# Gate square roots and norm roots as powers on GpSimd, and a rebuilt first stage, in a two-layer decoder trunk on one core

## Chip, cores, metric

One core of one Trainium2 chip. The metric is the device time of one execution in microseconds (us), lower is better. The core has a matrix engine (PE), a vector engine (DVE), a scalar engine (ACT) that computes functions from loadable tables, GpSimd (POOL), and SP, which here only issues transfers from HBM.

## The reference

The input x has 256 rows of 1024. Layer 0 is a gated linear recurrence, layer 1 causal attention with 8 heads of 128 (one block of 256 keys, so plain causal softmax). Cut to what matters here:

```python
def _rmsnorm(x, g):
    y = xf * lax.rsqrt(jnp.mean(xf * xf, axis=-1, keepdims=True) + EPS)
    return (y * g.astype(jnp.float32)).astype(x.dtype)
...
    r = jax.nn.sigmoid((_block_diag(u, w_a) + b_a).astype(jnp.float32))
    gi = jax.nn.sigmoid((_block_diag(u, w_x) + b_x).astype(jnp.float32))
    log_a = -RG_C * r * jax.nn.softplus(-lam.astype(jnp.float32))
    a = jnp.exp(log_a)
    b_in = jnp.sqrt(-jnp.expm1(2.0 * log_a)) * (gi * u.astype(jnp.float32))
    _, hs = lax.associative_scan(_lin_combine, (a, b_in), axis=1)
    y = hs.astype(h.dtype) * jax.nn.silu(g)
    return y @ w_out
...
    x = x + gate[:, None, :] * y
```

Every sub-layer reads `RMSNorm(x) * (1 + scale(c)) + shift(c)`, where shift, scale and gate are products of silu(c) with `mod_w`. A last norm gives the output.

## The kernel before

All weights come through SP as 512 KB blocks in the order of the string `ORDER`, each into one of `NRAW` raw buffers. Every large product runs as three products of split numbers: `split_into` makes a rounded part (`hi`, a cast on ACT or DVE) and the rest (`lo`, a subtraction on DVE), and PE multiplies hi by hi, hi by lo and lo by hi into one PSUM bank.

The program is first recorded as a list of operations. A planner (`Plan`) gives each a cost from a formula, simulates the engines, and so sets the order of the instructions on each engine and, where an operation may run on either, whether ACT or DVE takes it. It tries 80 random variations of its priorities and keeps the best. The order on each engine is then fixed; semaphores do the rest.

The stages, with the names that the prediction uses:

- **First stage.** The two halves of x (`xr`) are squared and summed on ACT (`sq_a`), `rms` turns the sums into 1/root (`rv_a`, `rn_a`, `rt_a`, `ry_a`), `xn_a` is the normed half, and PE transposes it (`tp_a`). Meanwhile silu(c) is made from `c8` and the first 128 columns of shift and scale are computed by `mod_one` (banks `gvm0s`, `mc_m0s`, result `sg4m0s`). `mod_apply` forms h (`hrm`, `h_hi`, `h_lo`) and `u_rows` starts the product u = h W (bank `u`). `warm` matmuls fill PE before that.
- **Gates.** u is convolved (`uc`); two groups of four 128-channel slices (j = 0, 1) follow. PE makes `pa` and `px`, ACT the sigmoid (`rr`), tanh (`tx`), then Exp (`aq`, the decay a) and Tanh of p4 times r (`rr` again). With t that tanh, the factor under the root is proportional to t, and the root is applied to it, times (1 + a).
- **Scan and output.** DVE multiplies the root into `wgx`, runs four scans, multiplies with the SiLU path (`sg`), splits into `y_hi` and `y_lo`; PE multiplies with `wo` (bank `r_wo`). The gate row is spread over partitions by POOL (`gate_g`), and x1 follows.
- **Layer 1.** Norm `b`, the keys and values (`v`, `k`), attention, output product (`r_wp`), norm `f` and the output `ot`.

In the gates the root is a table function on ACT, followed by a product on DVE:

```python
        A.activation(qg, rr, AF.Sqrt, scale=0.0625)
        V.scalar_tensor_tensor(wg[:, js], ag, 1.0, wg[:, js], ALU.add, ALU.mult)
        V.tensor_mul(wg[:, js], qg, wg[:, js])
```

ACT holds one set of function tables at a time: Sigmoid, Sqrt, Ln and the set of Exp and Tanh each need an `ACT_TABLE_LOAD` when the function changes.

Of the kernel before, what the change touches and what calls it, by code (L numbers as in the profile page):

```python
# [10 lines left out]
F32 = mybir.dt.float32  # L11
# [15 lines left out]
NRAW = 11  # L27
NSPL = 4
NWARM = 16
NWARM2 = 4  # L30
SUM0 = 3
# [16 lines left out]
def blocks():  # L48
# [55 lines left out]

def packed(inputs):
# [14 lines left out]
class Plan:  # L120
# [7 lines left out]
    SETS = {AF.Exp: "e", AF.Tanh: "es", AF.Sigmoid: "s", AF.Sqrt: "q", AF.Ln: "l"}  # L128
# [157 lines left out]

    def _forward(self, urge):
# [12 lines left out]
        while len(seq) < n:  # L300
# [52 lines left out]
        return max(fin), start, eng, sorted(range(n), key=lambda i: (start[i], i))  # L353

# [7 lines left out]
    def order(self):  # L362
# [15 lines left out]
        rnd = random.Random(self.SEED)  # L378
        for _ in range(self.ROUNDS):
            part, far = rnd.choice((0.003, 0.01, 0.05, 0.3)), rnd.choice((500, 3000, 10000))  # L380
            other = [u + rnd.gauss(0, far) if rnd.random() < part else u for u in urge]
            got = self._forward(other)
            if got[0] <= best[0]:
                best, urge = got, other
# [8 lines left out]
    ROUNDS, SEED = 80, 4  # L393
# [35 lines left out]
def kernel(ctx: ExitStack, tc: tile.TileContext, x, c, mod_b, norm_g, rg_conv_w, rg_conv_b,  # L429
                       rg_b_a, rg_b_x, rg_lambda, kv_norm_g, kv_mod_b, final_norm_g, pack, out):  # L430
# [16 lines left out]
    x, c, out = x[0], c[0], out[0]  # L447
# [13 lines left out]
    def split_into(raw, hi, lo):  # L461
        plan.copy(hi, raw)
        V.tensor_sub(lo, raw, hi.bitcast(F32))


    def wsplit(name):
        while len(halves) <= windex[name]:
# [5 lines left out]
            split_into(t, hi, lo)  # L473
# [86 lines left out]
    th = const.tile([KT, P], F32, name="cth")  # L560
    A.activation(th, c8, AF.Tanh, scale=0.5)
    V.scalar_tensor_tensor(c8, th, 1.0, c8, ALU.add, ALU.mult)
    pt = bank("pt_c")
    PE.transpose(pt[:, 0:KT], c8, ident[0:KT, 0:KT])
    csB = const.tile([P, KT, 32], F32, name="csB")
    V.tensor_scalar(csB, pt[:, 0:KT].unsqueeze(2).broadcast_to([P, KT, 32]), 0.5, None, ALU.mult)
    csT = const.tile([P, KT], F32, name="csT")
    V.tensor_scalar(csT, pt[:, 0:KT], 0.5, None, ALU.mult)
# [3 lines left out]


    def rms(nm, parts, early=None):
        bias, nbias = eps, neps
        for i, row in enumerate(parts):
            w = row.shape[-1]
            sq = tmp.tile([P, w], F32, tag="xn" if w > 512 else "tg", name=f"sq_{nm}{i}")
            if early is not None and i == 0:
                A.activation(sq[0:early.shape[0], 0:1], early, AF.Sqrt, scale=0.0)  # L580
            ss = small.tile([P, 1], F32, tag="ss", name=f"ss_{nm}{i}", bufs=4)
            A.activation(sq, row, AF.Square, accum_out=ss)
            if i < len(parts) - 1:
                b = small.tile([P, 2], F32, tag="rb", name=f"rb_{nm}{i}", bufs=4)
                V.tensor_scalar(b[:, 0:1], ss, 1.0 / D, bias, ALU.mult, ALU.add)
# [201 lines left out]
    for k in range(2):  # L787
        mod_apply("m0", k, 1, m0s[k], xnT, h0_h, h0_l)
        u_rows(k)
# [353 lines left out]
```

## Time and profile before

| | us |
|---|---|
| median of 3 runs | 257.39 (257.09 to 258.31) |
| profiled execution | 257.7 |
| its span, first to last instruction | 255.7 |
| PE busy | 242.2 (95%) |
| DVE busy | 208.8 (82%) |
| ACT busy | 161.2 (63%) |
| POOL busy | 18.3 (7%) |

The profile is of one execution; 2.0 us of its time lie around the span. Busy PE includes filler matmuls. Idle time of an engine is put down to what released it.

### The profile page before, as it was taken

The numbers are of one execution on the slowest core, as the hardware profiler recorded it, in microseconds if no ns is written. First come the engines' busy times: TensorE is split into PE (matmuls) and PEld (weight loads), VectorE is DVE, ScalarE is ACT, GpSimd is POOL, SyncE is SP. The second block draws the span as 40 slices with busy tenths as digits, with TensorE's granted clock in tenths as the row PEclk, the third lists the DMA queues.
The fourth block names the chain that finished last, engine by engine and source line by source line (L and its number), as shares of the span: only waits on it lengthen the run. The fifth ranks groups of instructions, "written<-read, shape, count | busy, mean of one in ns | idle before, by whom it ended". The sixth has DMA issues, their size and how long they took to land.

```text
span 255.7 us, 4865 instructions
## 1 busy us (share of the span) xinstructions
PE 242.2 (95%) x1823; PEld 215.7 (84%) x1823; DVE 208.8 (82%) x378; ACT 161.2 (63%) x288; POOL 18.3 (7%) x31
## 2 busy tenths in 40 slices
PE   8899999999999996997999999999999999999970
PEld 7697799999897874865898898999999998889870
DVE  2773799899969999999898999973766789798483
ACT  7662755595799995079943385863537365786242
POOL 8100000000000033000000000010000000005030
PEclk9999999999999999999999999999999999999996
DMA  6999999992697879999999999986897520000003
GB/s 214 410 417 420 413 420 417 420 415 91 238 352 314 309 270 360 419 396 383 420 316 378 395 393 415 416 299 261 253 354 292 173 82 3 1 0 3 1 17 147
DMA packets 20695, 72.24 MB, mean 283 GB/s; under 512 B 2728, under 2 KB 3008, under 8 KB 20672
## 3 DMA queue, kind: packets, MB, share of 16 engines
q1 hardware_dynamic: 19840, 71.15, 71.9%
q0 software_dynamic: 688, 0.59, 0.9%
q8 instruction: 14, 0.23, 0.4%
q10 hardware_dynamic: 144, 0.20, 0.2%
q14 instruction: 9, 0.07, 0.1%
HBM read 70.87 MB, written 1.05 MB: 281 GB/s over the span
## 4 chain that ended last, share of the span: by engine, by line
PE 77%; ACT 12%; DVE 7%; issue 2%; DVEq 0%; ACTq 0%
PE u L409 9%; PE g L409 9%; PE v L409 9%; PE r_wp L409 6%; PE ga L409 5%; PE pj_wkb L409 5%; PE pj_wqb L409 5%; PE q L409 5%; PE k L409 4%; PE r_wo L409 3%; DVE x L409 3%; PE sc L409 3%; ACT L409 3%; PE warm L409 2%; PE pj_wgc L409 2%
## 5 line engine op out<-in xcount | busy, mean ns | idle before, releaser
L409 ACT ACT_TABLE_LOAD x14 | 18.0, 1283 | 1.0 <-PEq L1126 0.7
L409 PE MATMUL u<-h_lo,wu_hi 128*128 128x256 f32 x64 | 18.1, 285 | 0.0
L409 PE MATMUL u<-h_hi,wu_lo 128*128 128x256 f32 x64 | 18.1, 284 | 0.0
L409 PE MATMUL g<-h_hi,wgb_hi 128*128 128x256 f32 x64 | 18.0, 283 | 0.0
L409 PE MATMUL g<-h_lo,wgb_hi 128*128 128x256 f32 x64 | 18.0, 283 | 0.0
L409 PE MATMUL u<-h_hi,wu_hi 128*128 128x256 f32 x64 | 17.8, 288 | 0.0
L409 PE MATMUL g<-h_hi,wgb_lo 128*128 128x256 f32 x64 | 17.8, 283 | 0.0
L409 DVE SCALAR_TENSOR_TENSOR maccg<-g,csT,maccg 128x1024 f32<-128x1024 f32 x12 | 15.3, 1278 | 1.3 <-DMA g<-in_pack_dram 1.3
L409 POOL DMA_DIRECT2D row_g<-gsg x8 | 4.6, 582 | 142.1 <-issue 142.1
L409 PE MATMUL r_wp<-wp_hi,o_hi 128*128 128x512 f32 (+1 forms) x40 | 14.6, 364 | 0.0
L409 PE MATMUL r_wp<-wp_lo,o_hi 128*128 128x512 f32 (+1 forms) x40 | 14.2, 354 | 0.0
L409 PE MATMUL r_wo<-wo_hi,y_hi 128*128 128x512 f32 x32 | 12.4, 397 | 1.6 <-ACT y_hi L169 1.6
L409 PE MATMUL r_wp<-wp_hi,o_lo 128*128 128x512 f32 (+1 forms) x40 | 13.8, 350 | 0.0
L409 PE MATMUL v<-wv_hi,hk_hi 128*128 128x512 f32 x32 | 12.3, 394 | 1.3 <-ACT hk_hi L169 1.3
L409 PE MATMUL r_wo<-wo_hi,y_lo 128*128 128x512 f32 x32 | 12.3, 394 | 0.4 <-DVE y_lo L409 0.4
L409 DVE TENSOR_TENSOR wgb_lo<-wgb,wgb_hi 128x1024 fp32r<-128x1024 f32 x8 | 9.8, 1222 | 3.5 <-ACT wgb_hi L169 3.5
L409 PEld LDWEIGHTS u<-h_lo,wu_hi 128*128 128x128 f32 x64 | 12.2, 191 | 0.4 <-issue 0.4
L409 PEld LDWEIGHTS u<-h_hi,wu_lo 128*128 128x128 f32 x64 | 12.2, 191 | 0.4 <-issue 0.4
L409 PE MATMUL v<-wv_lo,hk_hi 128*128 128x512 f32 x32 | 12.5, 391 | 0.0
L169 ACT CAST wgb_hi<-wgb 128x1024 fp32r<-128x1024 f32 x8 | 8.4, 1048 | 6.3 <-PE g L409 3.7
L409 PE MATMUL r_wo<-wo_lo,y_hi 128*128 128x512 f32 x32 | 12.4, 397 | 0.0
L409 PEld LDWEIGHTS g<-h_hi,wgb_hi 128*128 128x128 f32 x64 | 12.3, 192 | 0.0
(306 smaller groups left out, 868.6 us busy)
## 6 DMA issues: line engine op xcount, KB each, us to landing
g<-in_pack_dram SPq DMA_DIRECT2D x16, 512.0 KB, 5.0
wu<-in_pack_dram SPq DMA_DIRECT2D x8, 512.0 KB, 10.0
wo<-in_pack_dram SPq DMA_DIRECT2D x8, 512.0 KB, 6.5
mkh<-in_pack_dram SPq DMA_DIRECT2D x8, 512.0 KB, 6.3
mkc<-in_pack_dram SPq DMA_DIRECT2D x8, 512.0 KB, 6.9
wv<-in_pack_dram SPq DMA_DIRECT2D x8, 512.0 KB, 7.3
m1h<-in_pack_dram SPq DMA_DIRECT2D x8, 512.0 KB, 5.2
m1c<-in_pack_dram SPq DMA_DIRECT2D x8, 512.0 KB, 5.3
```

The source lines that it names most:

```text
L169: self.record(eng, fn, args, kw, lambda f=f, args=args, kw=kw: f(*args, **kw))
L409: self.plan.record(self.name, fn, args, kw, lambda: f(*args, **kw))
```

## The change

- The root in the gates is no longer an ACT function. POOL raises `rr` to the power 0.5 in two pieces of 128x512 per group (a `tensor_tensor` with the constant `half`), and DVE multiplies each piece into `wgx` with the factor 0.25.
- In every norm, ACT's Sqrt, the reciprocal and one Newton step on DVE are replaced by an addition on DVE and a 128x1 power of -0.5 on POOL; the partial sums of a row in several pieces are added on POOL. So the Sqrt table is loaded nowhere.
- The first stage: one transfer of a 128x160 array brings all small vectors, already transposed on the host (before: ten transfers on POOL's and SP's queues, and three PE transposes). The first 128 columns of shift and scale come from 16 matmuls of one column each (`mod_first`), h of these columns is made straight from the transposes' PSUM banks, and the next three sets of 128 columns come by `mod_one`. The first two transposed banks come from the pool `accp`. x comes in two transfers, 28 warm matmuls stand where 16 were, and `NRAW` is 12.
- The planner's search is replaced by a list of 26 seeds (`KEEP`); `ORDER` is changed a little, and its formula for the landing of transfers.
- The last norm: DVE multiplies by `fgB` into `ot`, not in place.

```diff
+    def mod_first(nm, m, gain, bias, both, new):
+        cp = new(f"mc_{nm}{m}")
+        for w in (1, 0):
+            t = got[f"{nm}{'hc'[w]}{m // 2}_{m % 2}"]
+            for kt in range(KT):
+                PE.matmul(cp[:, w:w + 1], t[:, kt], csT[:, kt:kt + 1], start=(w == 1 and kt == 0),
+                          stop=(w == 0 and kt == KT - 1), skip_group_check=True)
...
-    def rms(nm, parts, early=None):
-        bias, nbias = eps, neps
+    def rms(nm, parts, spare=None):
+        bias = EPS
         for i, row in enumerate(parts):
...
-            A.activation(sq, row, AF.Square, accum_out=ss)
+            A.activation(sq, row, AF.Square, scale=D ** -0.5, accum_out=ss)
             if i < len(parts) - 1:
...
-                V.tensor_scalar(b[:, 0:1], ss, 1.0 / D, bias, ALU.mult, ALU.add)
-                V.tensor_scalar(b[:, 1:2], ss, -0.5 / D, nbias, ALU.mult, ALU.add)
-                bias, nbias = b[:, 0:1], b[:, 1:2]
+                b = small.tile([P, 1], F32, tag="rb", name=f"rb_{nm}{i}", bufs=4)
+                G.tensor_scalar(b, ss, bias, None, ALU.add)
+                bias = b
         v = small.tile([P, 1], F32, tag="rv", name="rv_" + nm)
-        A.activation(v, ss, AF.Sqrt, bias=bias, scale=1.0 / D)
-        nv = small.tile([P, 1], F32, tag="rn", name="rn_" + nm)
-        V.tensor_scalar(nv, ss, -0.5 / D, nbias, ALU.mult, ALU.add)
+        V.tensor_scalar(v, ss, bias, None, ALU.add)
         y = small.tile([P, 1], F32, tag="ry", name="ry_" + nm)
-        V.reciprocal(y, v)
-        t = small.tile([P, 1], F32, tag="rt", name="rt_" + nm)
-        V.scalar_tensor_tensor(t, y, nv, y, ALU.mult, ALU.mult)
-        V.scalar_tensor_tensor(y, t, 1.5, y, ALU.add, ALU.mult)
+        G.tensor_tensor(y, v, mhalf, ALU.pow)
         return y
...
+    t4 = m0s[0]
+    hr = tmp.tile([P, S], F32, tag="hr", name="hr_first", bufs=3)
+    for s in range(ST):
+        sl = slice(s * P, (s + 1) * P)
+        A.activation(h0_h[:, 0, sl], tps[s][0][:, 0:P], AF.Identity, bias=t4[:, 0, 0:1], scale=t4[:, 0, 1:2])
+        V.tensor_scalar(hr[:, sl], tps[s][0][:, 0:P], t4[:, 0, 1:2], t4[:, 0, 0:1], ALU.mult, ALU.add)
+    V.tensor_sub(h0_l[:, 0], hr, h0_h[:, 0].bitcast(F32))
...
-        A.activation(qg, rr, AF.Sqrt, scale=0.0625)
         V.scalar_tensor_tensor(wg[:, js], ag, 1.0, wg[:, js], ALU.add, ALU.mult)
-        V.tensor_mul(wg[:, js], qg, wg[:, js])
+        for i in range(2):
+            sl, ws = slice(2 * i, 2 * i + 2), slice(4 * j + 2 * i, 4 * j + 2 * i + 2)
+            G.tensor_tensor(qg[:, sl], rr[:, sl], half.unsqueeze(2).broadcast_to([P, 2, S]), ALU.pow)
+            V.scalar_tensor_tensor(wg[:, ws], qg[:, sl], 0.25, wg[:, ws], ALU.mult, ALU.mult)
...
-    c8 = const.tile([KT, P], F32, name="c8")
-    SP.dma_start(c8, c.rearrange("(k p) -> k p", p=P))
+    vT = const.tile([P, NV], F32, name="vT")
+    SP.dma_start(vT, vecs)
...
-            plan.after = (last,)
             for q in parts:
-                V.tensor_mul(x2[:, s, q], x2[:, s, q], fgB[:, q])
-            plan.after = ()
-            A.activation(ot[:, 0:CUT], x2[:, s, 0:CUT], AF.Identity, scale=rstd)
-            V.tensor_scalar(ot[:, CUT:], x2[:, s, CUT:], rstd, None, ALU.mult)
+                V.tensor_mul(ot[:, q], x2[:, s, q], fgB[:, q])
+            A.activation(ot[:, 0:CUT], ot[:, 0:CUT], AF.Identity, scale=rstd)
+            V.tensor_scalar(ot[:, CUT:], ot[:, CUT:], rstd, None, ALU.mult)
```

What stands on the engines now. On ACT, at the first gate group, before the change: `aq<-rr,n` is Exp, `rr<-rr,p` Tanh, `aq<-rr` the root, `rr<-pa` the sigmoids of the second group.

```order
L409 ACT_TABLE_LOAD
L409 ACTIVATE aq_340<-rr_341,n_295 128x256 x4
L409 ACTIVATE rr_341<-rr_341,p_294 128x256 x4
L409 ACTIVATE tx_352<-px_351,hbx 128x256
L409 ACT_TABLE_LOAD
L409 ACTIVATE aq_340<-rr_341 128x1024
L409 ACT_TABLE_LOAD
L409 ACTIVATE tx_355<-px_354,hbx 128x256
L409 ACT_TABLE_LOAD
L409 ACTIVATE rr_349<-pa_350,pbT 128x256 x2
```

The same place after the change.

```order
L434 ACT_TABLE_LOAD
L434 ACTIVATE aq_328<-rr_329,n_295 128x256 x3
L434 ACTIVATE tx_340<-px_339,hbx 128x256
L434 ACTIVATE rr_329<-rr_329,p_294 128x256
L434 ACTIVATE aq_328<-rr_329,n_295 128x256
L434 ACTIVATE rr_329<-rr_329,p_294 128x256 x3
L434 ACTIVATE tx_340<-px_339,hbx 128x256
L434 ACTIVATE tx_343<-px_342,hbx 128x256 x2
L434 ACT_TABLE_LOAD
L434 ACTIVATE rr_337<-pa_341,vT 128x256
```

The root and two of the four table loads of this piece are gone, and the tanh of the second group runs in between.

On DVE, at the second gate group, before the change (`aq<-aq,wgx` are the scans, `wo_2_lo` splits a weight block).

```order
L409 SCALAR_TENSOR_TENSOR wgx<-aq_348,wgx 128x1024
L409 SCALAR_TENSOR_TENSOR sg_328<-tg_pj_wgc_356_361,pj_wgc_356 128x512
L169 CAST wo_2_hi<-wo_2_135 128x1024
L409 TENSOR_TENSOR wo_2_lo<-wo_2_135,wo_2_hi 128x1024
L409 TENSOR_TENSOR wgx<-aq_348,wgx 128x1024
L409 SCALAR_TENSOR_TENSOR aq_348<-aq_348,wgx 128x256 x3
L409 TENSOR_TENSOR sg_328<-aq_348,sg_328 128x512
L409 SCALAR_TENSOR_TENSOR aq_348<-aq_348,wgx 128x256
L409 TENSOR_TENSOR sg_328<-aq_348,sg_328 128x512
L409 TENSOR_TENSOR y_lo<-sg_328,y_hi 128x512
L409 TENSOR_TENSOR wo_3_lo<-wo_3_136,wo_3_hi 128x1024
```

The same place after the change; `wgx<-aq` of 128x512 are the products with the two powers.

```order
L434 SCALAR_TENSOR_TENSOR wgx<-aq_336,wgx 128x1024
L434 SCALAR_TENSOR_TENSOR wgx<-aq_336,wgx 128x512 x2
L434 SCALAR_TENSOR_TENSOR aq_336<-aq_336,wgx 128x256 x2
L434 TENSOR_TENSOR wo_2_lo<-wo_2_136,wo_2_hi 128x1024
L434 TENSOR_TENSOR sg_316<-aq_336,sg_316 128x512
L434 SCALAR_TENSOR_TENSOR aq_336<-aq_336,wgx 128x256 x2
L434 TENSOR_TENSOR wo_3_lo<-wo_3_135,wo_3_hi 128x1024
L434 TENSOR_TENSOR y_lo<-sg_316,y_hi 128x512
L434 TENSOR_TENSOR sg_316<-aq_336,sg_316 128x512
L434 TENSOR_TENSOR wo_2_lo<-wo_2_134,wo_2_hi 128x1024
L434 TENSOR_TENSOR y_lo<-sg_316,y_hi 128x512
```

The one product of 128x1024 has become two of 128x512, and two weight splits stand among the scans where one stood behind them.

On PE, in the first stage, before the change, from the last two of its `gvm0s` matmuls to the filler.

```order
L409 MATMUL gvm0s_233<-m0c_0_84,csB 32x128 x2
L409 MATMUL tp_a_245<-ident,xn_a_243 128x128 x4
L409 MATMUL tp_a_256<-ident,xn_a_255 128x128 x2
L409 MATMUL mc_m0s_235<-sel_222,partm0s_234 128x2
L409 MATMUL tp_a_256<-ident,xn_a_255 128x128 x2
L409 MATMUL ga_269<-ones 128x128
L409 MATMUL tp_a_257<-ident,xn_a_255 128x128 x4
```

And after the change, from the first warm matmuls to the first product.

```order
L434 MATMUL warm<-ones 128x128 x20
L434 MATMUL tp_a_233<-ident,xn_a_232 128x128 x4
L434 MATMUL tp_a_234<-ident,xn_a_232 128x128 x4
L434 MATMUL warm<-ones 128x128 x2
L434 MATMUL tp_a_239<-ident,xn_a_238 128x128 x4
L434 MATMUL tp_a_240<-ident,xn_a_238 128x128 x4
L434 MATMUL mc_m_242<-csT,m0c_0_82 128x1 x8
L434 MATMUL mc_m_242<-csT,m0h_0_83 128x1 x8
L434 MATMUL warm<-ones 128x128 x6
L434 MATMUL ga_251<-ones 128x128 x4
L434 MATMUL u_246<-h_hi,wu_hi 128x256 x2
```

All transposes now stand ahead of the first modulation, whose 16 one-column matmuls (`mc_m`) stand right in front of the fillers and u.

## Rows read from the trace of the kernel before

**Rows 1.** The page, part 1: busy us (share of the span) and instructions of each engine.
```profile
PE 242.2 (95%) x1823; PEld 215.7 (84%) x1823; DVE 208.8 (82%) x378; ACT 161.2 (63%) x288; POOL 18.3 (7%) x31
```

**Rows 2.** Windows: stretch, length, busy time and instructions by engine, clock, DMA.
```profile
14.30:61.30 47.00, 47.00 (x424) 43.84 (x421) 38.47 (x82) 27.72 (x40) 0.00 (x0) 1.00 0.97 396
...
96.00:102.00 6.00, 4.00 (x24) 2.39 (x21) 5.97 (x8) 3.49 (x5) 2.20 (x1) 1.00 0.97 361
...
102.00:118.00 16.00, 14.42 (x118) 10.16 (x117) 15.59 (x32) 8.12 (x18) 0.00 (x0) 1.00 1.00 397
...
118.00:240.00 122.00, 122.00 (x875) 113.20 (x876) 99.63 (x155) 74.56 (x143) 4.39 (x6) 1.00 0.65 245
```

**Rows 3.** Timeline of the start: start us, duration us, instruction, idle before.
```profile
4.59 1.06 ACT L409 ACTIVATE sq_a<-xr 128x1024 f32<-128x1024 f32 x1 [0.64 <-DMA xr<-in_x_dram]
...
5.55 0.19 ACT L409 ACTIVATION_READ_ACCUMULATOR sq_a<-xr 128x1 f32 x1
...
8.30 0.75 DVE L169 TENSOR_SCALAR xn_a<-xr,ry_a 128x1024 f32<-128x1024 f32 x1
...
9.62 1.15 ACT L169 ACTIVATE xn_a<-xr,ry_a 128x1024 f32<-128x1024 f32 x1 [1.97 <-DVE ry_a L409]
...
11.41 0.28 PE L409 MATMUL mc_m0s<-sel,partm0s 128*128 128x2 f32 x2
...
12.63 0.60 ACT L169 ACTIVATE hrm<-xnT,sg4m0s 128x256 f32<-128x256 f32 x1
...
14.30 0.39 PE L409 MATMUL u<-h_hi,wu_hi 128*128 128x256 f32 x1
```

**Rows 4.** Chain that ended last, two pieces of the first stage.
```profile
9.11 0.66 PE tp_a L409 x4
...
11.58 0.12 PE mc_m0s L409 x2
```

**Rows 5.** Waits: who waited for whom, total us, times, longest us.
```profile
DVE wu_hi L169 <- DMA wu<-in_pack_dram: 3.9, 1, 3.9
```

**Rows 6.** Timeline of ACT at the first gate group.
```profile
74.24 1.28 ACT L409 ACT_TABLE_LOAD   x1
...
75.53 1.06 ACT L409 ACTIVATE aq<-rr 128x1024 f32<-128x1024 f32 x1
...
76.61 1.28 ACT L409 ACT_TABLE_LOAD   x1
```

**Rows 7.** Timeline, all engines, end of the second gate group.
```profile
93.36 1.23 DVE L409 TENSOR_TENSOR wgx<-aq,wgx 128x1024 f32<-128x1024 f32 x1 [0.22 <-ACT aq L409]
...
97.09 0.62 ACT L169 CAST y_hi<-sg 128x512 fp32r<-128x512 f32 x1 [0.94 <-DVE sg L409]
...
97.76 0.49 PE L409 MATMUL r_wo<-wo_hi,y_hi 128*128 128x512 f32 x1 [1.56 <-ACT y_hi L169]
...
99.09 2.20 POOL L409 PARTITION_BROADCAST gate_g<-row_g  x1 [6.64 <-issue]
...
100.04 1.65 DVE L409 TENSOR_TENSOR y_lo<-sg,y_hi 128x512 fp32r<-128x512 f32 x1
...
101.75 0.50 PE L409 MATMUL r_wo<-wo_hi,y_lo 128*128 128x512 f32 x1 [0.43 <-DVE y_lo L409]
```

**Rows 8.** Groups of POOL and DVE instructions: count, busy us, mean ns.
```profile
L409 POOL TENSOR_TENSOR ot<-x,fgB 128x512 f32<-128x512 f32 x2 | 2.6, 1289 | 8.3 <-PE r_wp L409 7.6 <-DVE x L409 0.6
...
L409 DVE TENSOR_TENSOR y_lo<-sg,y_hi 128x512 fp32r<-128x512 f32 x4 | 3.7, 929 | 0.0
```

**Rows 9.** Timeline, smallest POOL instruction of the run.
```profile
0.24 0.10 POOL L1126 MEMSET const-float32-0.0<- 128x1 f32 x1 [0.24 <-issue]
```

**Rows 10.** Timeline of PE where the second layer starts.
```profile
117.98 0.50 PE L409 MATMUL v<-wv_hi,hk_hi 128*128 128x512 f32 x1 [1.33 <-ACT hk_hi L169]
```

**Rows 11.** Timeline, last norm and last scaling.
```profile
250.00 0.30 ACT L409 ACTIVATE rv_f<-ss_f,rb_f 128x1 f32<-128x1 f32 x1 [0.22 <-DVE rb_f L409]
...
251.17 0.62 ACT L409 ACTIVATE ot<-x,ry_f 128x384 f32<-128x384 f32 x1 [0.88 <-DVE ry_f L409]
```

More of the change, by code (lines that the diff above doesn't have):

```diff
@@ L102, with columns @@
 BLOCKS = blocks()
+VECTORS = ("c", "mod_b", "norm_g", "rg_conv_w", "rg_conv_b", "rg_b_a", "rg_b_x", "rg_lambda", "kv_norm_g", "kv_mod_b")
+NV = 160
+def columns(inputs):
+    import numpy as np
+    return np.concatenate([inputs[n].reshape(-1, P) for n in VECTORS]).astype(np.float32).T
 def packed(inputs):
@@ L353, in _forward, with _shake @@
         return max(fin), start, eng, sorted(range(n), key=lambda i: (start[i], i))
+    @staticmethod
+    def _shake(urge, k):
+        rnd = random.Random(k)
+        part, far = rnd.choice((0.001, 0.003, 0.01, 0.05, 0.3)), rnd.choice((500, 3000, 10000))
+        return [u + rnd.gauss(0, far) if rnd.random() < part else u for u in urge]
     def _on(self, i, e):
@@ L376, in order @@
         best = self._forward(urge)
[L378 to L384, printed above, removed]
+        if KEEP:
+            for k in KEEP:
+                urge = self._shake(urge, k)
+            best = self._forward(urge)
         self.span, self.start, eng, seq = best
@@ L567 @@
     csT = const.tile([P, KT], F32, name="csT")
-    V.tensor_scalar(csT, pt[:, 0:KT], 0.5, None, ALU.mult)
-    def rms(nm, parts, early=None):
-        bias, nbias = eps, neps
+    V.tensor_scalar(csT, cs2, 0.5, None, ALU.mult)
+    def rms(nm, parts, spare=None):
+        bias = EPS
         for i, row in enumerate(parts):
[L577 to L580, printed above, removed]
+            sq = tmp.tile([P, row.shape[-1]], F32, tag="tg", name=f"sq_{nm}{i}") if spare is None else spare
@@ L785, in u_rows @@
         gemm_T(ub, wh, wl, h0_h, h0_l, kt)
[L787 removed]
+    t4 = m0s[0]
+    hr = tmp.tile([P, S], F32, tag="hr", name="hr_first", bufs=3)
+    for s in range(ST):
+        sl = slice(s * P, (s + 1) * P)
+        A.activation(h0_h[:, 0, sl], tps[s][0][:, 0:P], AF.Identity, bias=t4[:, 0, 0:1], scale=t4[:, 0, 1:2])
+        V.tensor_scalar(hr[:, sl], tps[s][0][:, 0:P], t4[:, 0, 1:2], t4[:, 0, 0:1], ALU.mult, ALU.add)
+    V.tensor_sub(h0_l[:, 0], hr, h0_h[:, 0].bitcast(F32))
+    first = len(plan.ops) - 1
+    m0s.append(mod_one("m0", 1, *args0))
+    wh, wl = wsplit("wu_0", (first,))
+    for i, (w, h) in enumerate(((wh, h0_h), (wh, h0_l), (wl, h0_h))):
+        for m in range(KT):
+            PE.matmul(ub[m // 2][:, (m % 2) * S:(m % 2 + 1) * S], w[:, m * P:(m + 1) * P], h[:, 0],
+                      start=(i == 0 and m % 2 == 0), stop=False, skip_group_check=True)
+    started = len(plan.ops) - 1
+    for k in range(1, 4):
         mod_apply("m0", k, 1, m0s[k], xnT, h0_h, h0_l)
+        if k < 3:
+            m0s.append(mod_one("m0", k + 1, *args0))
+        else:
+            nxt = mod_pair("m0", 2, *args0)
         u_rows(k)
[L790 to L796 removed]
+        if k % 2:
+            pair_T(gb, "wga", h0_h, h0_l, k // 2)
+    pbT = vT[:, KT + 64:]
     cwT = pbT[:, 0:32].rearrange("p (j k) -> p j k", j=4)
@@ L1130 @@
     inputs["pack"] = packed(inputs)
+    inputs["vecs"] = columns(inputs)
     for name in _INS:
```

139 lines of the change are left out of this document (70 added, 69 removed).

## Prediction, made before the changed kernel ran

> **What bounds the kernel now.** I read the page's busy times first: PE works in 242.2 of 255.7 us, DVE in 82%, ACT in 63%, POOL in 7% [rows 1]. So a faster ACT or DVE gains only where PE stands still, or where PE's work is filler. The table of windows then says where that is. From the first product to 61.3 us PE is busy in all of 47.00 us, and from 118 to 240 in all of 122.00 [rows 2]: there the edits can give nothing but an earlier start. PE is idle in 2.00 of the 6 us from 96 to 102 and in 1.58 of the 16 us from 102 to 118 [rows 2]. Before 14.30 it runs fillers and small work; the first product of u starts at 14.30 [rows 3]. At the end the last ot starts on ACT at 251.17, when the matmuls are long done [rows 11]. Four places are left: start, second gate group, norm b, tail.
>
> What ends each wait: in the gates PE waits 1.56 us for ACT's y_hi at 97.76 and 0.43 us for DVE's y_lo at 101.75 [rows 7]; PE waits 1.33 us for hk_hi before the first v [rows 10]; ACT's last ot waits 0.88 us for the root [rows 11].
>
> **The start.** The first half of x is squared from 4.59 us, for 1.06 us; the read of its sum ends at 5.55 + 0.19 = 5.74, so a half takes 1.15 us [rows 3]. Now both halves are squared whole: done at 4.59 + 2 x 1.15 = 6.89. Then an addition on DVE and a 128x1 power on POOL. The trace has no power. Its nearest small row on POOL is 0.10 us for a fill of 128x1 [rows 9], the nearest two-input row 1.29 us for 128x512 [rows 8]; I take 0.6 us for addition and power with their hand-overs, with 0.2 and 1.4 as ends. That gives 7.5. The scaling to xn on DVE takes 0.75 [rows 3]: 8.25 (before, the second half was scaled on ACT from 9.62 for 1.15 us, to 10.77 [rows 3]). Eight transposes behind it, four in 0.66 us [rows 4], take 1.32: 9.6. Then the 16 one-column matmuls. The nearest row is mc_m0s, one two-column matmul in two records: 0.12 us in the chain [rows 4], 0.28 us as the timeline has it [rows 3]. I take 0.12, since the chain counts what a matmul adds to the next: 1.9 us, to 11.5; the other end is 16 x 0.28 = 4.5. Scale and shift columns and h_hi from PSUM are three short ACT instructions, no longer together than two of the 0.60 us hrm [rows 3]: 1.2, to 12.7. So the first product starts 1.6 us earlier, with ends of 2.3 earlier (power and hand-overs at 0.2, columns 0.3 quicker) and 1.8 later (power at 1.4, columns at 4.5). All work behind it is the same products, on a PE that is never idle [rows 2], so the shift is kept up to the gates. The dropped transposes of c and of the vectors, and the transfers on SP's and POOL's queues ahead of them, are covered by the transfer of x, which ends the wait of the first square [rows 3]; uncovered, each transpose would be worth about 0.17 us, a quarter of the row of four [rows 4]. More fillers cost nothing in front of a wait.
>
> **The gates.** At j = 0, ACT loses a table load of 1.28, the root of 1.06 and a second load of 1.28 [rows 6]: 3.6 us, which pulls the sigmoids of j = 1 forward. At j = 1 it loses a load and a root, 2.34 us, and DVE's product of 1.23 us [rows 7] becomes two of half the size. What comes in: two powers of 128x512 per group on POOL. Low end 1.29 us each, the multiply of the same shape on that engine [rows 8]; high end 3.9, an estimate as three such passes, for a logarithm, a product and an exponential. I take the low end, the one row with the same engine, shape and two inputs. On the path of j = 1 then stand 2 x 1.29 = 2.6 in place of 1.28 + 1.06, about equal, but the first half can be scanned while the second is raised, and the group starts earlier by part of the 3.6 us. Against this, DVE's order at j = 1 puts one weight split ahead of sg and another behind the second pair of scans, so the later y_hi and y_lo gain less than the first. PE cannot use more than its idle time: 2.00 us [rows 2]. I take 1.5 of it.
>
> One row speaks against this. DVE's y_lo of j = 1 took 1.65 us while POOL spread the gate row [rows 7]; the group's mean of four is 0.93 us [rows 8], so the other three took (3.7 - 1.65) / 3 = 0.7. An instruction of DVE that reads two tensors was held for about 1 us beside one on POOL. The Trainium skill, SBUF — State Buffer, section Who interferes with whom, says that such a DVE instruction and a POOL instruction that reads SBUF exclude each other, and that whichever starts first keeps the port to its end. By that rule the trace's y_lo is explained, and the sum for the gates would be nearly nothing, as worked out under the second rival.
>
> gate_g now stands behind the powers on POOL's queue; it was spread from 99.09 to 101.29 [rows 7], and x1 needs it only after the last r_wo, so this is covered by the output products; uncovered it would be one power, 1.29 us.
>
> **Norms b and f.** ACT's root of 0.30 us [rows 11] and four short DVE steps go; one addition and one power come. At b, an addition of partial sums on POOL and both scalings on ACT come too, and the transposes stand behind all of gvmk. I count 0, between 0.5 gained and 1.0 lost (power at 1.29). At the tail the path from the root's start to ot is 251.17 - 250.00 = 1.17 us [rows 11]; addition and power at 0.6 give 0.6 back, and DVE's product with fgB, now ahead of the last residual addition, takes some: 0.4 gained, between 0.8 gained and 0.3 lost. The table loads that go elsewhere lie beside a busy PE [rows 2]: nothing.
>
> **Sum.** 1.6 + 1.5 + 0 + 0.4 = 3.5 us from the profiled 257.7: 254.2. The median lies 0.3 below the profiled execution, so 253.9.
>
> **Rivals.**
>
> *The power is dear.* For: a power has more steps than a multiply, and no row times one. Against: no row shows more than 2.20 us for anything of this size on POOL [rows 7], and that was 128x1024. Each us above 1.29 counts twice at j = 1, where PE already waits, and about once at j = 0, whose first y_hi PE needs as soon as its own products run out: 3 us of time for each. At 3.9 us that is 2.6 x 3 = 7.8 lost: 253.9 + 7.8 = 261.7. It decides from 1.29 + 3.5 / 3 = 2.5 us per power: above, the kernel is slower than before.
>
> *DVE and POOL take turns.* For: the y_lo row. Nearly every DVE instruction of the gates reads two tensors, so each power holds DVE, or waits for it. At j = 1 this puts 2 x 1.29 on top of DVE's work, against the 2.34 that ACT gave back and the 1.23 that was one product before and after: the gates gain nothing, or lose 0.5. Time: 253.9 + 1.5 + 0.5 = 255.9. Against: each group has only two powers.
>
> *Transfers bound the start.* The DMA is at 0.97 of its capacity from 14.3 to 61.3 [rows 2] and DVE waited 3.9 us for a block of wu [rows 5]. If a block comes no earlier, PE's earlier start runs into it and the 1.6 us are lost: 255.5. Against: PE was never idle in that stretch, and a product block feeds PE longer than it takes to land.
>
> **Chances and range.** The forecast 0.55, turns 0.20, a dear power 0.17, transfers 0.08. The measurement tells about 0.5%, 1.3 us: faster means below 256.1. The forecast gives 0.50 to faster and 0.05 to same, turns 0.10 and 0.09 with 0.01 slower, transfers 0.08 to faster, the dear power 0.03 to same and 0.14 slower: 0.68, 0.17, 0.15. The range goes from 250.8 (2.3 at the start, 2.0 in the gates, 0.5 at b, 0.8 at the tail, and 1.0 for waits that the new order may remove) to 258.4, which takes in turns, transfers and the lower part of a dear power; 0.13 to 0.2 lies outside.
>
> **What would show it.** Right: u's first product near 12.7; POOL's TENSOR_TENSOR of 128x512 near 1.3 us; no Sqrt load; the idle of PE before the second group's r_wo below 0.5 us; the tail from the last sum to ot near 0.6 us. The start is wrong if mc_m takes much over 2 us or xn waits for the power. Turns would show as y_lo, scans or wgx well above their 0.7 us beside a power. A power above 2.5 us makes the prediction wrong as a whole.

## The result, and the profile after

The changed kernel took 594.0 us (median of 4 runs, 592.6 to 595.8), the kernel before 257.4 beside it: a ratio of 2.305, with an interval of 2.300 to 2.311. I had predicted 253.9. The profiled execution spans 590.8 us. Times of runs are medians; where the executions of a kernel fell into two groups, those of the slower group are left out.

The page of the changed kernel: part 2 (busy tenths in 40 slices of 14.8 us, and the granted clock), the chain, and the costliest group.

```profile
PE   9999970000000000290000000000377999999992
...
POOL 2000069999999999579999999999610000000013
PEclk9999995555555555596555555555597999999997
...
POOL 56%; PE 35%; ACT 3%; issue 2%; DVE 2%; POOLq 0%; DVEq 0%; ACTq 0%
...
L434 POOL TENSOR_TENSOR aq<-rr,half 128x512 f32<-128x512 f32 x4 | 328.1, 82034 | 82.1 <-ACT rr L434 82.1
```

PE stands still in two holes, from the seventh to the sixteenth slice and from the nineteenth to the twenty-eighth, and POOL is busy in just these; 56% of the chain that ended last is POOL's. Behind that stands one group, four powers of 128x512 of 82.03 us each: 328 us, against a loss of 337. Where PE stood still its granted clock was 0.50, the lower of its two levels (1.2 GHz). The nearest row of before was 1.29 us [rows 8].

The timeline of POOL in the changed kernel (start, duration, instruction, idle before and what ended it).

```profile
79.56 164.27 POOL L434 TENSOR_TENSOR aq<-rr,half 128x512 f32<-128x512 f32 x2 [71.44 <-ACT rr L434]
254.48 163.81 POOL L434 TENSOR_TENSOR aq<-rr,half 128x512 f32<-128x512 f32 x2 [10.65 <-ACT rr L434]
...
425.92 3.53 POOL L434 PARTITION_BROADCAST gate_g<-row_g  x1 [5.67 <-issue]
440.41 0.25 POOL L434 TENSOR_SCALAR rb_b<-ss_b 128x1 f32<-128x1 f32 x1 [10.95 <-issue]
...
568.31 1.56 POOL L434 PARTITION_BROADCAST gate_g<-row_g  x1 [5.79 <-issue]
576.85 2.54 POOL L434 TENSOR_TENSOR ot<-x,fgB 128x512 f32<-128x512 f32 x2 [6.98 <-issue]
```

Each group's two powers follow each other without a gap. Then comes something that I had not looked for: after each spread of the gate row (PARTITION_BROADCAST) POOL stands still for 10.95 and 6.98 us, put down to "issue", which means that it waited for nothing that the profile shows.

The start of the changed kernel, timeline; below it the window from 14 to 16 us, whose columns behind POOL are the granted clock, the DMA share and GB/s.

```profile
7.55 0.56 POOL L434 TENSOR_TENSOR ry_a<-rv_a,mhalf 128x1 f32<-128x1 f32 x1 [0.93 <-DVE rv_a L434]
8.15 0.75 DVE L434 TENSOR_SCALAR xn_a<-xr,ry_a 128x1024 f32<-128x1024 f32 x1 [0.68 <-POOL ry_a L434]
...
9.77 1.04 PE L434 MATMUL tp_a<-ident,xn_a 128*128 128x128 f32 x8
...
10.64 1.84 PE L434 MATMUL mc_m<-csT,m0c 128*128 128x1 f32 x16
...
11.72 1.05 ACT L187 CAST wu_hi<-wu 128x1024 fp32r<-128x1024 f32 x1 [0.24 <-DMA wu<-in_pack_dram]
...
12.35 2.20 PE L434 MATMUL mc_m<-csT,m0h 128*128 128x1 f32 x16
...
14.41 2.91 PE L434 MATMUL warm<-ones 128*128 128x128 f32 x12
...
15.22 0.91 ACT L434 ACTIVATE h_hi<-tp_a,sg2m 128x128 fp32r<-128x128 f32 x2
...
17.99 0.48 PE L434 MATMUL u<-h_hi,wu_hi 128*128 128x256 f32 x2
```

```profile
14.00:16.00 2.00, 2.00 (x10) 2.00 (x11) 0.91 (x3) 1.13 (x3) 0.00 (x0) 0.50 1.07 430
```

The first product of u starts at 17.99; before it was 14.30 [rows 3], and I had said 12.7. From 14 to 16 us PE is busy at half its clock.

The end of the changed kernel, timeline.

```profile
584.90 0.21 DVE L434 TENSOR_SCALAR rv_f<-ss_f,rb_f 128x1 f32<-128x1 f32 x1 [0.60 <-ACT sq_f L434]
585.20 0.56 POOL L434 TENSOR_TENSOR ry_f<-rv_f,mhalf 128x1 f32<-128x1 f32 x1 [1.21 <-DVE rv_f L434]
585.80 0.62 ACT L434 ACTIVATE ot<-ot,ry_f 128x384 f32<-128x384 f32 x1 [1.35 <-POOL ry_f L434]
```

From the last root's input to ot 0.90 us pass (584.90 to 585.80), before 1.17 [rows 11]. ACT loads a table 7 times (x7 in its group of ACT_TABLE_LOAD, 9.0 us), before 14 times.

### The profile page after: what moved, and what is told of

Same layout as the page of the kernel before. It is cut to its first block, busy times and chain, and to the rows that moved or that the text cites. A ratio compares the mean times of both kernels' runs of the same rounds, so it can differ in the third digit from the quotient of the medians.

```text
span 590.8 us, 4920 instructions
## 1 busy us (share of the span) xinstructions
PE 253.3 (43%) x1874; PEld 226.7 (38%) x1874; DVE 206.5 (35%) x345; ACT 152.9 (26%) x277; POOL 348.9 (59%) x39
## 3 DMA queue, kind: packets, MB, share of 16 engines
HBM read 70.87 MB, written 1.05 MB: 122 GB/s over the span
## 4 chain that ended last, share of the span: by engine, by line
POOL 56%; PE 35%; ACT 3%; issue 2%; DVE 2%; POOLq 0%; DVEq 0%; ACTq 0%
POOL aq L434 56%; PE u L434 4%; PE g L434 4%; PE v L434 4%; PE r_wp L434 3%; PE ga L434 2%; PE pj_wkb L434 2%; PE pj_wqb L434 2%; PE q L434 2%; PE k L434 2%; PE warm L434 2%; PE sc L434 1%; PE pj_wgc L434 1%; PE r_wo L434 1%; PE oT L434 1%
## 5 line engine op out<-in xcount | busy, mean ns | idle before, releaser
L434 POOL TENSOR_TENSOR aq<-rr,half 128x512 f32<-128x512 f32 x4 | 328.1, 82034 | 82.1 <-ACT rr L434 82.1
L434 PE MATMUL r_wo<-wo_hi,y_hi 128*128 128x512 f32 x32 | 14.3, 467 | 318.7 <-ACT y_hi L187 318.7
L434 PEld LDWEIGHTS r_wo<-wo_hi,y_hi 128*128 128x128 f32 x32 | 6.8, 225 | 321.3 <-ACT y_hi L187 319.4
L434 DVE SCALAR_TENSOR_TENSOR wgx<-aq,wgx 128x512 f32<-128x512 f32 (+1 forms) x6 | 7.4, 1231 | 319.7 <-POOL aq L434 319.6
L434 ACT ACTIVATE rr<-pa,vT 128x256 f32<-128x256 f32 x8 | 3.2, 473 | 162.9 <-POOL aq L434 162.0
L187 ACT CAST y_hi<-sg 128x512 fp32r<-128x512 f32 x4 | 2.5, 632 | 160.6 <-DVE sg L434 160.6
L434 DVE SCALAR_TENSOR_TENSOR maccg<-g,csT,maccg 128x1024 f32<-128x1024 f32 x12 | 15.4, 1280 | 0.1
L434 PE MATMUL v<-wv_lo,hk_hi 128*128 128x512 f32 x32 | 12.7, 398 | 0.0
```

The lines of the kernel that those rows point to most:

```text
L187: self.record(eng, fn, args, kw, lambda f=f, args=args, kw=kw: f(*args, **kw))
L434: self.plan.record(self.name, fn, args, kw, lambda: f(*args, **kw))
```

## Experiments

Theory one: a power on GpSimd is paid by the column, and the four large ones are the loss. Its rivals were the operand that is read with stride zero (two), DVE holding GpSimd up (three), and another part of the change (four).

**e1, the power alone.** One instruction per case: `G.tensor_tensor(o, base, e, ALU.pow)`, also with `ALU.mult`, and one of 64 columns beside 16 DVE operations with two operands.

> A kernel of its own: it copies x to the output and computes nothing of the reference; beside the copy GpSimd runs powers and multiplies of several widths, exponents and operands, one after the other. In the changed kernel the 128x1 power took 0.57 us and the 128x512 power 82.0 us, which is 0.16 us for each further column. Theory one, the power is paid by the column: widths 1, 2, 8, 64, 256 and 512 take 0.57, 0.73, 1.7, 10.6, 41 and 82 us; a tile full of exponents, the exponents -0.5 and 2.0, and 16 partitions in place of 128 all take 82 us; a multiply with the same broadcast operand takes 1.3 us; 64 columns take the same 10.6 us with DVE quiet and with DVE busy. Theory two, the operand that is read with stride zero is what is slow: the tile full of exponents takes a few us, and the multiply with the broadcast operand tens of us. Theory three, DVE holds GpSimd up: 64 columns beside a quiet DVE are far below those beside a busy DVE.

Groups of POOL in e1 (count, busy us, mean ns, idle before):

```profile
L37 POOL TENSOR_TENSOR full<-base,e_half 128x512 f32<-128x512 f32 x1 | 82.1, 82132 | 0.0
L37 POOL TENSOR_TENSOR inv<-base,e_mhalf 128x512 f32<-128x512 f32 x1 | 82.1, 82132 | 0.0
L37 POOL TENSOR_TENSOR sq<-base,e_two 128x512 f32<-128x512 f32 x1 | 82.1, 82132 | 0.0
L37 POOL TENSOR_TENSOR part<-base,e_half 16x512 f32<-16x512 f32 x1 | 82.1, 82127 | 0.0
L37 POOL TENSOR_TENSOR w<-base,e_one 128x512 f32<-128x512 f32 x1 | 81.9, 81909 | 0.0
L37 POOL TENSOR_TENSOR w<-base,e_one 128x256 f32<-128x256 f32 x1 | 41.1, 41120 | 0.0
L37 POOL TENSOR_TENSOR w<-base,e_one 128x64 f32<-128x64 f32 x1 | 10.5, 10513 | 0.0
...
L37 POOL TENSOR_TENSOR mul<-base,e_one 128x512 f32<-128x512 f32 x1 | 1.0, 1028 | 0.0
```

Timeline of e1's end, the power of 64 columns and then a multiply, both beside DVE.

```profile
482.36 10.51 POOL L37 TENSOR_TENSOR busy<-base,e_one 128x64 f32<-128x64 f32 x1
...
482.76 10.14 DVE L60 TENSOR_TENSOR dve<-dve,dve 128x512 f32<-128x512 f32 x14
...
492.83 1.03 POOL L37 TENSOR_TENSOR mulbusy<-base,e_one 128x512 f32<-128x512 f32 x1
492.93 1.49 DVE L60 TENSOR_TENSOR dve<-dve,dve 128x512 f32<-128x512 f32 x1
```

Theory one holds. From 256 to 512 columns a power grows by 40.8 us, 0.159 us a column, and 64 columns fit that line. A full tile of exponents (`full`), other exponents (`inv`, `sq`) and 16 partitions (`part`) all cost the same 82 us; the multiply with the stride-zero operand takes 1.0. Beside DVE the power takes 10.5 us as before, and DVE's fourteen operations beside it take 0.69 us each, as one does alone (10.14 us with the 0.03 between them). So neither held the other, and theories two and three fall. The multiply behind it is another matter: the one DVE operation that began beside it took 1.49 us.

**e2, e3, e4: the rest of the change.** The edits are in `after` and, for e4, in `before`. e3 leaves the square root out. e2 and e4 were planned anew, e3 keeps the order of the changed kernel. Cut:

```diff
-            G.tensor_tensor(qg[:, sl], rr[:, sl], half..., ALU.pow)
+            A.activation(qg[:, sl], rr[:, sl], AF.Sqrt)              # e2
+            G.tensor_tensor(qg[:, sl], rr[:, sl], half..., ALU.mult) # e3
-        A.activation(qg, rr, AF.Sqrt, scale=0.0625)                  # e4, in before
+        for i in range(2): G.tensor_tensor(qg[:, 2*i:2*i+2], rr[:, 2*i:2*i+2], half..., ALU.pow)
```

> The changed kernel with its four gate powers put back as square roots on ACT (two of 128x512 per group); norm powers, new first stage and fillers stay. Theory one, the four powers are the whole loss: 594 minus 4 x 82 us of powers, minus the time in which PE was slow after its two stops, plus ACT's roots and table loads: 255 to 260 us. Theory four, another part of the change (first stage, norm powers, order) loses more than 2% by itself: above 262 us.

> The changed kernel with the four powers replaced by multiplies of the same operands, shapes, engine and place, so the gates hold no square root and the output is another one. Theory one, the operation itself: the four instructions take 1.3 us each and the time is 252 to 259 us, near what I predicted for the change. Theory two, the broadcast operand, or the place and order: the four stay at tens of us and the time above 400 us.

> The kernel before with nothing changed but the gate roots: two powers of 128x512 per group on GpSimd in place of ACT's root. Theory one: 257 plus 4 x 82 plus a few us at the slower clock, less the two roots: 585 to 597 us, whatever the first stage and the norms do. Theory four, a large share of the loss belongs to the rest of the change: below 575 us.

e2 took 270.6 us (in brackets, here and below, the ratio to the kernel before and its 95% interval: 1.049, 1.045 to 1.052), e3 272.8 (1.059, 1.056 to 1.061), e4 578.5 in one execution, with the same four powers:

```profile
L409 POOL TENSOR_TENSOR aq<-rr,half 128x512 f32<-128x512 f32 x4 | 328.1, 82030 | 76.7 <-ACT rr L409 76.7
```

So the gate powers alone cost 578.5 - 257.3 = 321 us in the old kernel, and the change without their price costs 272.8 - 257.3 = 15.4; together 593.8, the measured 594.0. Theory one explains 95% of the loss, and theory four the rest: without dear powers the change is still 6% slower, where I had expected 1.4% faster. The next runs are on these 15 us.

In e3, POOL's spread and its next instruction, and the ACT row that gives this instruction its operand:

```profile
106.05 3.74 POOL L434 PARTITION_BROADCAST gate_g<-row_g  x1 [5.87 <-issue]
...
112.63 0.19 ACT L434 ACTIVATION_READ_ACCUMULATOR sq_b<-x 128x1 f32 x1
...
120.91 0.25 POOL L434 TENSOR_SCALAR rb_b<-ss_b 128x1 f32<-128x1 f32 x1 [11.12 <-issue]
```

The sum of the first half is read by 112.82, the addition `rb_b` starts at 120.91: 11.1 us after the spread, 8.1 after its operand. Theory five: between a spread and ordinary arithmetic GpSimd is held, as if it had to fetch code. Theory six: the wait has another cause.

**e7, the switch alone.** Arithmetic, spreads and 128x1 powers on POOL, with quiet transfers and then beside 48 loads.

> A kernel of its own: it copies x to the output and computes nothing of the reference; GpSimd alternates plain arithmetic, the spread of a row over the partitions (128x1024) and a 128x1 power, first with quiet transfers and then beside 48 loads of 512 KB. Theory five: about 6 us pass ahead of each spread that follows arithmetic and some 7 us ahead of the first arithmetic after a spread, none between two spreads or two arithmetic instructions, and the gaps grow beside the loads, to 11 us or so. Theory six: gaps below 1 us everywhere.

Timeline of POOL in e7:

```profile
17.13 1.30 POOL L42 PARTITION_BROADCAST oquiet<-rquiet  x1 [5.60 <-issue]
25.34 0.25 POOL L43 TENSOR_SCALAR aquiet<-base 128x1 f32<-128x1 f32 x1 [6.91 <-issue]
25.58 0.59 POOL L44 TENSOR_TENSOR aquiet<-aquiet,half 128x1 f32<-128x1 f32 x1
31.92 1.30 POOL L45 PARTITION_BROADCAST oquiet<-rquiet  x1 [5.75 <-issue]
33.10 1.30 POOL L46 PARTITION_BROADCAST oquiet<-rquiet  x1
41.24 0.25 POOL L47 TENSOR_SCALAR aquiet<-base 128x1 f32<-128x1 f32 x1 [6.84 <-issue]
...
58.86 1.30 POOL L42 PARTITION_BROADCAST odma<-rdma  x1 [9.75 <-issue]
71.72 0.25 POOL L43 TENSOR_SCALAR adma<-base 128x1 f32<-128x1 f32 x1 [11.55 <-issue]
```

Theory five holds, in both directions: 5.6 to 5.8 us ahead of a spread that follows arithmetic, 6.9 ahead of arithmetic that follows a spread, nothing between two of a kind; beside the loads 9.75 and 11.55. The Trainium skill, GPSIMD Engine Reference, section 2.1 Instruction dispatch, says that the first call of freshly loaded code pays about 6 us without an instruction in the profile. The quiet gaps agree with that; that the price comes back at each alternation, and nearly doubles beside full transfers, these rows show and that section does not. That it is code which is fetched is the page's word; the rows show the gap. In the changed kernel the gap goes with the transfers too: 10.95 us behind the first spread, where the DMA share was 1.03 (429.5 to 440.4 us), and 6.98 behind the second, where it was 0.00 (569.9 to 576.8).

**e5, e6, e8: parts of the change, planned anew.** e5 is `before` with norm roots as powers, e6 is e3 with norm b on ACT and DVE, e8 the first stage without any power.

> The kernel before with nothing changed but the norm roots: one 128x1 power on GpSimd in place of ACT's root and DVE's reciprocal and Newton step; gate roots and first stage as before. The multiply run showed GpSimd standing still for 11.1 us between its spreading of the gate row and its next arithmetic, with the operand there after 3. Theory five, GpSimd cannot start ordinary arithmetic until some 11 us after a spread, as if it had to fetch that code again: the spread of before ends at 101.3, so the first power of norm b starts near 112.4, where the root is now done at 112.0, and the time is 256.5 to 259. Theory six, a 128x1 power and its hand-overs are 0.6 us each and nothing else: the first power of norm b starts near 110, and the time is 255.5 to 257.2.

> The multiply run (so still no square root in the gates, another output) with norm b alone back on ACT and DVE, as before; norms a and f stay powers. Theory five (GpSimd held after the spread): from the end of the output product of layer 0 to the first product of v it took 14.7 us, before 7.9; now 8 to 9.5, and the time falls from 272.8 to 265 to 268. Theory six (the wait has another cause, such as the order of the work): the 14 us stay, and so does the time, within 2 us.

> The changed kernel with gate roots and norm roots all back on ACT and DVE (no power is left): what stays is the new first stage, the fillers and the order. Theory seven, the sixteen one-column matmuls leave TensorE so little to do that its clock falls from 2.4 to 1.2 GHz (the granted clock was 0.50 from 14 to 20 us in the run with the roots on ACT): the first product of u starts at 18 to 19 us, the product phase ends 5 to 6 us late, and the time is 262 to 268. Theory eight, the start costs nothing in the end, since transfers bound the stretch behind it: 255 to 259.

e5 took 262.0 us (1.020, 1.015 to 1.024), e6 280.2 (1.088, 1.082 to 1.094), e8 269.3 (1.046, 1.043 to 1.049): all three outside what I had written. The planner orders a changed list anew, and this covered the edit: in e6 the gate row's transfers were issued at 110.41 in place of 98.14 (e3), and x1 waited for the spread; in e8 33.8 us pass from the first product of pj_wgc to the first of r_wo, in before 26.0; in e5, with the old first stage, u's first product starts at 18.64. On norm b and on the start they decide nothing. From here I replaced only the call behind a planned operation, so that every other instruction keeps its place:

```diff
         G.tensor_tensor(y, v, mhalf, ALU.pow)
+        plan.ops[-1]["call"] = root   # ACT's root, DVE's reciprocal and Newton step
```

**e9 to e12, in a kept order.** e9 is the changed kernel with its four roots on ACT, e10 is e3 with norm b's arithmetic off GpSimd; e11 and e12 are `before` with powers in norms a and f, and in a, b and f.

> The changed kernel with each gate power replaced by ACT's square root at the very place that the planner gave the power; the order of every other instruction on every engine is that of the changed kernel (the earlier run with the roots on ACT was planned anew and so mixed a new order in). Theory one with the start and norm b as the rest of the loss: the four powers of 82 us go, ACT takes 0.6 us per root and a table load before and after most of them, and 265 to 273 us are left. Theory nine, the extra loss of the earlier run came from its new order: 257 to 261.

> The multiply run (so no square root in the gates, another output) with the arithmetic of norm b taken off GpSimd at the places where it stood: the sum of the two halves on DVE, the root on ACT, reciprocal and Newton step on DVE; all other instructions keep the order of the multiply run. Theory five, GpSimd is held for 11.1 us after the spread of the gate row (shown alone: 6.9 us with quiet transfers, 11.4 beside loads): xn_b starts near 117 and not at 122.1, and the time falls from 272.8 to 266 to 269. Theory six, something else holds norm b: the time stays above 271.

> The kernel before, in its own order, with a 128x1 power on GpSimd at the place of root, reciprocal and Newton step in norms a and f only. Theory ten, there the power is cheaper (0.57 us and hand-overs against ACT's 0.3 and four steps on DVE) and GpSimd is not held, since no spread lies shortly ahead: 0.3 to 1.0 us faster than before, 256.3 to 257. Theory five with the end as its place too: GpSimd's first arithmetic after the second spread is late: 257.5 to 260.

> As the run with powers in norms a and f, in the order of the kernel before, with norm b's two roots as powers too. Theory five: the first power of norm b cannot start before the spread's end plus some 11 us, 101.3 + 11.4 = 112.7, where the root was done at 112.0: 1 to 2.5 us slower than the run without. Theory six: the same time as that run or 0.5 less.

e9: 274.1 us (1.064, 1.061 to 1.067), 1 us above my range; so the new order was not what cost e2 its time. e10: 265.3 (1.030, 1.025 to 1.034), so 7.5 us less than e3 and just under the 266 to 269 of theory five. From the last product of r_wo to the first of v 10.2 us pass, in e3 14.7; from the end of r_wp to the end of the span 8.1, in e3 11.3, since the second spread follows its transfers after 1.25 us and not 5.91. These two stretches make 4.5 + 3.2 = 7.7. They are the better measure: in these two profiles the start differs as well (u's first product at 15.98 in e10, at 18.67 in e3), which the edit does not touch. e11: 257.6 (1.001, 0.999 to 1.002), no change where I expected a small gain. e12: 263.1 (1.022, 1.019 to 1.025), 5.5 us more than e11 with norm b's two powers as the only difference; I had expected 1 to 2.5.

POOL in e12, and then in e11:

```profile
99.68 2.20 POOL L409 PARTITION_BROADCAST gate_g<-row_g  x1 [6.64 <-issue]
113.09 0.59 POOL L607 TENSOR_TENSOR ry_b<-rv_b,mhalf 128x1 f32<-128x1 f32 x1 [11.22 <-DVE rb_b L409]
114.79 2.07 POOL L607 TENSOR_TENSOR ry_b<-rv_b,mhalf 128x1 f32<-128x1 f32 x1 [1.11 <-DVE rv_b L599]
...
240.90 1.30 POOL L409 PARTITION_BROADCAST gate_g<-row_g  x1 [5.81 <-issue]
249.25 2.68 POOL L409 TENSOR_TENSOR ot<-x,fgB 128x512 f32<-128x512 f32 x2 [7.04 <-DVE x L409]
```

```profile
98.49 1.56 POOL L409 PARTITION_BROADCAST gate_g<-row_g  x1 [5.54 <-issue]
...
233.75 1.45 POOL L409 PARTITION_BROADCAST gate_g<-row_g  x1 [1.22 <-DMA row_g<-gsg]
242.15 1.29 POOL L409 TENSOR_TENSOR ot<-x,fgB 128x512 f32<-128x512 f32 x1 [6.95 <-DVE x L409]
```

In e12 norm b's first power starts 11.2 us after the spread, as forecast, and the first product of v 2.6 us later than in e11 (121.04 against 118.46). About 1.5 of these are the second power's own: it took 2.07 us in place of 0.57, beside DVE's split of a weight block (wv_lo, 1.22 us from 114.63). The rest was not in my sum: since POOL now does arithmetic in the middle, the second spread has to wait 5.81 us too (1.22 in e11), so the spread, and ot behind it, come 7 us later, and the span ends 5.6 us later (261.3 against 255.7). In e11 and in before POOL does no arithmetic between the two spreads. Theory five is shown by removal (e10) and by addition (e12).

**e13 to e16: the first stage.** e13 is e10 with the sixteen one-column matmuls 32 columns wide. e14 is the new first stage with norm a by a power, with the gate roots and norms b and f as before; its order of transfers, its raw buffers and the product with fgB are those of the changed kernel. e15 is the same 32 wide, e16 the same with the old `mod_one` for the first columns.

```diff
-                PE.matmul(cp[:, w:w + 1], t[:, kt], csT[:, kt:kt + 1], ...)   # e13, e15
+                PE.matmul(cp[:, w], t[:, kt], csB[:, kt], ...)
-    m0s = [mod_first("m0", 0, *args0, both0, bank)]                          # e16
+    m0s = [mod_one("m0", 0, *args0)]
```

> The run e10 (multiplies for the gate powers, so another output; norm b off GpSimd) with one edit: the sixteen matmuls that make the first scale and shift columns move 32 equal columns each in place of one. In the rows a matmul of 128x1 and one of 32 columns take the same time, since their weights are as large. Theory seven, a matmul of one column gives TensorE too little to do and its clock falls: the granted clock stays at 1.00 from 12 to 20 us in every profile, and the median falls from 265.2 to 262 to 264. Theory eleven, the width does not matter (the clock falls with either, or by the wait that surrounds them): 264.5 to 266.5.

> The changed kernel's first stage, fillers and norm a by a power; gate roots, norms b and f as in the kernel before; the order planned with 80 tries as before. Theory seven, the start is late by 2.4 us with a full clock and by 5.8 with a halved one: 259 to 264. Theory eight, a late start is hidden by the transfers: 256.5 to 258.

> As e14 with the sixteen matmuls 32 columns wide. Theory seven: the clock stays at 1.00 and the time lies 1 to 3 us under e14. Theory eleven: the same as e14 within 1 us.

> As e14, with the first 128 columns of shift and scale computed in the old form (32 matmul records of 128 columns with 32 stationary ones, a copy and a matmul with sel). Theory seven: those cost less time on TensorE and keep its clock, so the first product of u starts at 13.5 to 14.5 us and the time is 255.5 to 258; if below 256, this version beats both kernels. Theory twelve, the rest of the new first stage is late by itself: above 259.

e13: 264.8 us (1.027, 1.023 to 1.030), the same as e10 within the intervals. e14: 260.9 (1.011, 1.005 to 1.016). e15: 258.6 (1.004, 1.002 to 1.007). e16: 257.6 (1.000, 0.998 to 1.001). So e14, e15 and e16 came out as theory seven had it, e13 as theory eleven had it. Windows from 14 to 16 us of e14 and of e15:

```profile
14.00:16.00 2.00, 2.00 (x10) 2.00 (x11) 0.93 (x3) 1.14 (x3) 0.00 (x0) 0.50 1.02 401
```

```profile
14.00:16.00 2.00, 2.00 (x21) 2.00 (x19) 1.44 (x4) 1.97 (x4) 0.00 (x0) 1.00 1.03 406
```

The new start costs 3.5 us, and all of it goes with its new way to make the first columns: with the old way (e16) nothing is lost, and nothing gained. These three were planned anew each, by 80 tries, so some of the 3.5 may be order. Part of the cost does not need the clock: in the profiles of e10 and e15, with PE at 1.00, the columns take 3.6 and 3.7 us (10.25 to 13.89, 10.04 to 13.70), and u's first product starts at 15.98 and 15.77, in before at 14.30. With the clock at 0.50 it starts at 17.99 to 18.67 (after, e2, e3, e9, e14).

Whether the width of the columns has to do with the fall of the clock stays open. e14's profile fell to 0.50 and e15's did not. But the intervals of the two overlap a little, and so do the mean clocks of their executions (0.977 to 0.990 and 0.978 to 0.996); the profiles of e8 and e10 kept 1.00 with one column; e13 did not differ from e10; and in e5, which has no one-column matmul, the clock fell at the same place, there after PE had stood idle for 1.5 of 2 us:

```profile
12.00:14.00 2.00, 0.47 (x5) 0.28 (x4) 1.88 (x3) 0.02 (x1) 0.00 (x0) 0.94 1.04 418
14.00:16.00 2.00, 2.00 (x10) 1.78 (x11) 1.13 (x2) 0.65 (x2) 0.00 (x0) 0.50 1.01 403
```

No version beat the kernel before.

## Why the prediction was wrong, point by point

- **The power of 128x512** is the step that failed: "Low end 1.29 us each ... high end 3.9, an estimate as three such passes ... I take the low end". It measured 82.0, 21 times my upper end. A multiply's row bounds a power from below only; the three passes were invented, and no row stood behind them. The mechanism of the rival "The power is dear" was right, and 82 us lies far beyond its turning point of 2.5. Its slope was not right: I charged 3 us of time per us of power, since the first group's first power should be covered; with 82 us no cover lasts, and all four counted (321 / (82.0 - 1.3) = 4.0).
- **Norms b and f, "I count 0, between 0.5 gained and 1.0 lost".** The power itself was sized nearly right: 0.57 us for 128x1 in most rows, about 0.9 with its addition, where I took 0.6. What failed is that I priced instructions, not their neighbours: norm b's arithmetic between two spreads costs 5.5 us in the old order (e12, some 1.5 of it the long second power) and 7.5 in the new (e10). The profile of before hinted at it: POOL's first spread there follows its transfers after 6.64 us of "issue" [rows 7].
- **The start, "1.6 us earlier".** 3.7 later. The root of the second half was done at 7.55 + 0.56 = 8.11, the second scaling at 8.90; I had 7.5 and 8.25. The eight last transposes ended at 10.81, not 9.6. The columns took 3.9 us, from 10.64 to 14.55, where I took 1.9 for 16 matmuls at 0.12: a matmul has two records here, and each costs that. My other end, 4.5, was nearer. "More fillers cost nothing in front of a wait" failed too: h_hi was there at 15.22 + 0.91 = 16.13 and the first block's wu_hi at 11.72 + 1.05 = 12.77, and PE, at a lowered clock, ran fillers until the first product at 17.99.
- **"So the shift is kept up to the gates"**: its sign turned, and it grew: u's first product is 4.4 us late in e3 and in e14, the first product of pj_wgc, which follows the u products, 5.7 and 5.1.
- **The gates without the price, 1.5 of PE's 2.00 us of idle time.** In e3, where the four instructions took 1.52 us each and no root is computed, 6.05 us of delay ahead of r_wo's first product became 5.03 at its last: 1.0 gained, against a start that was already late, where I took 1.5.
- **DVE and POOL take turns.** This rival rested on the y_lo row [rows 7], beside a spread. It holds beside a multiply: in e1 the DVE operation took 1.49 us for 0.69, and in e3 three DVE products of 128x512 that began beside a multiply took 1.53, 1.52 and 1.35 for 0.68. It does not hold through a power (e1). Only near a power's start is DVE late: in the changed kernel `wgx<-tx,uc`, begun 0.5 us behind the first power, took 1.53 us. The rule of the Trainium skill that I weighed there (SBUF — State Buffer, Who interferes with whom) would have put these in turn; for the multiply the measurement agrees, for a power and a DVE operation with two operands it says that they are not, but for the power's start.
- **The tail, "0.4 gained".** The path from the last root to ot did get 0.27 us shorter, where I took 0.57; but ot's product with fgB on POOL came only 6.98 us after the second spread; in e12 the end behind the last product of r_wp lost 3.1 us against e11.
- **Transfers bound the start** was not tested, since the start came later. The table loads fell from 14 to 7.

Open: of the 15.4 us beside the powers, e10 assigns 7.5 to norm b with its tail and e14 3.5 to the start; some 4 are not assigned by a run. The profiles of before and e3, 17.1 us apart, say where the time lies: 4.4 at u's first product, 1.4 more up to pj_wgc, 0.7 given back in the gates, 6.8 from there to v's first product, 1.7 up to the last of r_wp, 3.5 behind it. In e10's profile 2.3 of the 6.8 and 1.5 of the 1.7 are still there, though POOL does no arithmetic in norm b. I put them down to the new order of the work, which no run shows; PE's clock fell there once more, to 0.76 from 118 to 125 us.

## What to carry to other kernels

An operation that no row of the trace shows has no upper bound from its neighbours: run it alone first, at two widths, before a change rests on it; one probe gave 0.41 us + 0.16 us per column, and the whole answer. An instruction on GpSimd is priced with its neighbours on the queue, since plain arithmetic on both sides of a spread costs the gap each way, 5.6 to 6.9 us here and more beside full transfers. And when a planner sets the order, compare variants in a kept order, or the order is what is measured.

## What was not expected of the hardware

- A power on GpSimd: 0.57 us for 128x1 and 82.0 for 128x512, 0.159 us per column, whatever the exponent, its layout and the partitions (16 or 128). Beside a power of 64 columns DVE's two-operand work went on at 0.69 us each; beside a multiply it took 1.49. One 128x1 power took 2.07 us beside a DVE split (e12).
- Changing between a spread and arithmetic on GpSimd: 5.6 to 6.9 us with quiet transfers, 9.75 to 11.55 beside loads (e7).
- PE's granted clock fell to 0.50 while PE was busy, in the stretch of one-column matmuls and fillers, in the profiles of after, e2, e3, e9 and e14, and stayed at 1.00 in those of e8 and e10. e14's six executions had mean clocks from 0.977 to 0.990, so it may differ from one execution of a program to the next; each has one profile, which does not show it.
